# New order shifts for the projection stage and layer 1's attention of a two-layer decoder, and the compressed keys turned in four operations instead of eight

## The chip, the cores and the metric

The kernel runs on one core of a Trainium2 chip, as one execution with all inputs and the output in device memory. The metric is device time in microseconds (us). Before the change three runs gave a median of 2461.87 us (2460.61 to 2462.18).

A core has five engines that run at once, each through its own list of instructions in order: TensorE (PE, matmuls and transposes), VectorE (DVE), ScalarE (ACT), GpSimd (POOL), and SyncE (SP), which here issues the transfers between device memory and the core's on-chip memory. An instruction waits, on semaphores, until what it reads is written and what it overwrites is read; everything behind it on its engine waits with it. In the profile "PE busy" is matmul time, "PEclk" the TensorE clock that was granted (1.00 is full speed).

## The reference

A batch of one, 1024 tokens of width 1024, two layers, float32. Layer 0 is native sparse attention, layer 1 forgetting attention; each layer also has four heads that attend to 256 memory tokens, an output projection and a convolutional FFN (width 2816). Cut to what matters here:

```python
# layer 0: projections and the compressed keys
proj = h @ w_in                      # queries, 6 x 2 groups of keys/values, gates, memory queries
blocks = u[:, idx] + pos_emb         # 63 blocks of 32 tokens, stride 16
flat = blocks.transpose(...).reshape(B, n_cmp, G, L_CMP * dh)
compress = gelu(flat @ w1 + b1) @ w2 + b2
kc = rope(compress(k_cmp), cmp_end)  # rope: [x1*cos - x2*sin, x2*cos + x1*sin]
vc = compress(v_cmp)
# layer 1: forgetting attention, causal in chunks of queries
s = q @ k.T * scale + dcum[t] - dcum[s]
o = masked_softmax(s, causal) @ v
```

Then `x = x + concat(o_mix, o_mem) @ w_o`, `x = x + conv_ffn(rms_norm(x))` for each layer, and a last norm.

## The kernel before

**Arithmetic.** Every float32 operand of a projection is split into an upper and a lower part, and `mm3` (L320, matmuls at L324 to L326) forms upper x upper, upper x lower and lower x upper. The upper part of a weight is a copy on ACT, the lower a subtraction on DVE or POOL (tiles `wh`, `wl`, from `wr`, where the transfer lands; 3 `wr`, 4 pairs `wh`/`wl`). Products go to PSUM: two wide buffers `psa` (1024 columns) and four `psb` (512).

**Stages**, in us of the profiled span: 0 to 154 the projections of layer 0; 154 to 590 its attention; 590 to 1150 its output projection and FFN; 1150 to 1420 down projection, norm and layer 1's first projections; 1420 to 1780 layer 1's attention; 1780 to 2464 the output projection, FFN and final norm of layer 1.

**What sets the order.** The projection stage and the two attentions are lists of tasks given to class `Plan` (L50). A task names an engine, an assumed duration (for instance 1.36 us for six matmuls, 0.69 us for a 512-wide DVE product), the tasks it follows, the buffers it takes and gives back, and a priority. `Plan.run` walks through assumed time while the program is built: a free engine takes the ready task with the lowest priority number whose buffers are free. The sequence that comes out is written down as each engine's program and is not altered when the chip runs it. The table `SHIFT` adds half of its number, in the units of the priority, to single tasks:

```python
if self.auto and not key:
    key = ("t", len(self.tasks))
if key:
    prio += 0.5 * self.shift.get(key[0], {}).get(key[1], 0)
```

`SHIFT["p"]` belongs to the projection stage, with tasks by their number; `SHIFT[0]` and `SHIFT[1]` to the attentions of the layers, by a letter for the kind of task and the number of its unit (s0 scores, m0 row maxima, e0 exponentials, n0 normalising, t transposes of the probabilities, h and l their upper and lower parts, v values, d loads of queries, keys and values, f fillers: the projections of layer 1 that are still to be done, w their weights, x loads of the output projection's operand, y its weights).

**The projection stage** (`proj_tasks`) holds the normed input `hT` of both halves of the tokens, multiplies it with the columns for values, keys and queries, turns queries and keys by RoPE on DVE (L1170) and POOL, and has two side chains. `compress_tasks` (L1276) is called for kind 0 (keys) and kind 1 (values): a projection into `psa`, scaling on DVE (L1317), placing the blocks with their positions into `kk` (L1332 on DVE, L1327 on POOL), their split into `m` (L1338 ACT, L1341 DVE), 16 steps of `mm3` with the weights w1 (the 128x256 matmuls `psb<-m,wh`, weights split at L1360 and L1363), the bias (L1379, DVE, tile `ch`), gelu (L1389, ACT), two transposes (L1384, PE), the split into `cth` (L1391 ACT, L1392 DVE), the matmul with w2, and a bias (L1401, tile `cres`). For the keys follow `rotate()` (L1409 to L1417, eight DVE operations of 128x32, tiles `crt` and `cdup`) and a transpose (L1421). The memory tokens' keys and values (`mem_tasks`, weights at L1541 and L1544, split of the operand at L1527) and memory queries (`mem_queries`, scaled at L1470) run in between.

**Layer 1's attention** (`planned` with `l=1`) goes through units of one head and one half of the queries. A unit loads its keys (`kk`, `ky`), queries (`qq`, two buffers; `qx`, one buffer for each half of the queries, L2003) and values (`vv`), forms scores in `psa` (L409, two matmuls of each width: 64 rows with the head's numbers, 80 with decay), reads them on DVE (L439: adds the mask, finds the maximum, frees `psa`), takes exponentials on ACT (L452), normalises on POOL, transposes the probabilities (L523), splits them (L534 ACT, L537 DVE, tiles `pt`) and multiplies with the values (L547). Between these PE has fillers: the projections of layer 1's queries and keys (`psb<-hT,wh` and `psb<-wh,hT` of 128x512, six to a task), whose results go to device memory (`qd`, `kd`) and come back as queries and keys. Row sums of heads go out by `ob` (L668) and come back as the output projection's operand (`wr<-o`, L694).

## Time and profile before

| what | number |
|---|---|
| median of 3 runs | 2461.87 us (2460.61 to 2462.18) |
| profiled execution, its own time | 2465.3 us |
| its span, first to last instruction | 2463.5 us, mean granted clock 0.998 |
| PE busy | 2425.6 us, 98% of the span |
| DVE, ACT, POOL busy | 72%, 54%, 42% |
| projection stage (0 to 154 us) | PE busy 144.94 us, DVE 109.62, ACT 76.78, POOL 88.42 |
| layer 1's attention (1420 to 1780 us) | PE busy 351.56 us, DVE 198.15, ACT 209.52, POOL 173.00 |

A row of a stretch reads: its limits, its length, then PE, weight loads, DVE, ACT and POOL busy us with the number of instructions, the granted clock, the share of the transfer engines and GB/s. A row of a timeline reads: start, duration, engine, line, operation, output and inputs, shape, count, and in brackets the idle time before it with what ended it. A row of waits reads: engine, tile and line that waited, what it waited for, us in total, how often, the longest.

### The profile page before, as it was taken

The numbers are of one execution on the slowest core, as the hardware profiler recorded it, in microseconds if no ns is written. First come the engines' busy times: TensorE is split into PE (matmuls) and PEld (weight loads), VectorE is DVE, ScalarE is ACT, GpSimd is POOL, SyncE is SP. The second block draws the span as 40 slices with busy tenths as digits, with TensorE's granted clock in tenths as the row PEclk, the third lists the DMA queues.
The fourth block names the chain that finished last, engine by engine and source line by source line (L and its number), as shares of the span: only waits on it lengthen the run. The fifth ranks groups of instructions, "written<-read, shape, count | busy, mean of one in ns | idle before, by whom it ended". The sixth has DMA issues, their size and how long they took to land.

```text
span 2463.5 us, 35014 instructions
## 1 busy us (share of the span) xinstructions
PE 2425.6 (98%) x12233; PEld 2042.4 (83%) x12233; DVE 1767.5 (72%) x2785; ACT 1330.4 (54%) x2466; POOL 1027.7 (42%) x964
## 2 busy tenths in 40 slices
PE   9989999999999999999999999999999999999998
PEld 8878888887888888888889888887778888888887
DVE  5888887875867887887665346556577878788766
ACT  5468887883444554454454256666345544444444
POOL 3765654782344554510003245437234545541001
PEclk9999999999999999999999999999999999999999
DMA  8772243556223333385335559568622333339423
GB/s 310 247 241 95 86 131 104 175 161 224 94 90 98 99 112 98 111 304 166 95 122 171 169 168 259 170 187 267 215 86 86 113 97 111 104 97 317 167 90 127
DMA packets 271888, 379.76 MB, mean 154 GB/s; under 512 B 24050, under 2 KB 139602, under 8 KB 271682
## 3 DMA queue, kind: packets, MB, share of 16 engines
q1 hardware_dynamic: 271712, 377.53, 47.2%
q8 instruction: 96, 1.57, 0.3%
q14 instruction: 80, 0.66, 0.1%
HBM read 256.67 MB, written 122.16 MB: 154 GB/s over the span
## 4 chain that ended last, share of the span: by engine, by line
PE 89%; DMA 4%; DVE 3%; ACT 2%; issue 1%; POOL 1%; SPq 0%; POOLq 0%; ACTq 0%; DVEq 0%
PE psa L324 13%; PE psa L325 13%; PE psa L326 13%; PE psb L324 10%; PE psb L326 10%; PE psb L325 10%; PE psa L409 6%; PE psb L523 6%; PE psb L547 6%; DMA qx<-qd 1%; PE psb L1768 1%; DVE pt L537 0%; DMA wr<-in_w_mem_kv_dram 0%; DVE m L1527 0%; DMA wr<-o 0%
## 5 line engine op out<-in xcount | busy, mean ns | idle before, releaser
L2349 DVE SCALAR_TENSOR_TENSOR v<-u,cw,v 128x1023 f32<-128x1023 f32 (+1 forms) x176 | 273.9, 1556 | 68.7 <-ACT v L2347 68.5
L537 DVE TENSOR_TENSOR pt<-psb,pt 128x512 fp32r<-128x512 f32 (+2 forms) x380 | 243.1, 660 | 67.7 <-ACT pt L534 62.3
L2347 ACT ACTIVATE v<-u,cw 128x1024 f32<-128x1024 f32 x88 | 109.6, 1246 | 310.2 <-DVE u L2336 297.1
L245 ACT ACTIVATE wh<-wr 128x512 fp32r<-128x512 f32 (+1 forms) x202 | 147.1, 729 | 233.2 <-PE psa L326 121.7
L547 PE MATMUL psb<-pt,vv 128*128 128x512 f32 (+2 forms) x864 | 262.6, 363 | 3.3 <-DVE pt L537 3.0
L534 ACT ACTIVATE pt<-psb 128x512 fp32r<-128x512 f32 (+2 forms) x380 | 212.4, 575 | 92.6 <-PE psb L523 72.7
L246 DVE TENSOR_TENSOR wl<-wr,wh 128x512 fp32r<-128x512 f32 (+1 forms) x202 | 186.6, 925 | 94.7 <-ACT wh L245 94.4
L292 POOL TENSOR_TENSOR rs<-ss,consts 128x1 f32<-128x1 f32 x28 | 17.1, 611 | 519.1 <-DVE ss L290 519.1
L324 PE MATMUL psa<-hT,wh 128*128 128x512 f32 x592 | 231.1, 391 | 0.1
L325 PE MATMUL psa<-hT,wh 128*128 128x512 f32 x592 | 230.4, 389 | 0.0
L326 PE MATMUL psa<-hT,wl 128*128 128x512 f32 x592 | 230.4, 389 | 0.0
L409 PE MATMUL psa<-kk,qq 128*128 128x512 f32 (+4 forms) x792 | 175.0, 336 | 6.8 <-DVE stat L439 2.2
L439 DVE CUSTOM_DVE_ANT_0 ps<-psa,caub 128x128 f32<-128x128 f32 (+1 forms) x192 | 139.1, 750 | 39.8 <-PE psa L409 32.2
L2242 POOL TENSOR_TENSOR ws<-wr 128x512 f32<-128x512 f32 x44 | 75.1, 1708 | 216.9 <-DMA wr<-in_w_up_dram 185.8
L452 ACT ACTIVATE ps<-ps,stat 128x128 f32<-128x128 f32 (+1 forms) x192 | 148.0, 775 | 32.4 <-DVE stat L439 31.9
L547 PEld LDWEIGHTS psb<-pt,vv 128*128 128x128 f32 x864 | 147.8, 189 | 18.1 <-DVE pt L537 4.4
L523 PE MATMUL psb<-consts,ps 128*128 128x128 f32 x928 | 145.0, 275 | 3.3 <-DVE pt L537 1.5
L324 PE MATMUL psa<-hx,wh 128*128 128x512 f32 x368 | 144.0, 392 | 0.4 <-ACT u L2339 0.4
L325 PE MATMUL psa<-hx,wh 128*128 128x512 f32 x368 | 143.6, 390 | 0.0
L326 PE MATMUL psa<-hx,wl 128*128 128x512 f32 x368 | 143.3, 389 | 0.0
L409 PEld LDWEIGHTS psa<-kk,qq 128*128 128x128 f32 x792 | 125.0, 191 | 22.1 <-DVE stat L439 6.2
L324 PE MATMUL psb<-wh 128*128 128x512 f32 x352 | 137.4, 390 | 0.1
(360 smaller groups left out, 6928.2 us busy)
## 6 DMA issues: line engine op xcount, KB each, us to landing
wr<-in_w_up_dram SPq DMA_DIRECT2D x88, 512.0 KB, 3.8
wr<-gd SPq DMA_DIRECT2D x154, 256.0 KB, 2.9
gd<-v SPq DMA_DIRECT2D x88, 256.0 KB, 2.1
qq<-qd SPq DMA_DIRECT2D x72, 256.0 KB, 4.0
gd<-gs SPq DMA_DIRECT2D x66, 256.0 KB, 2.3
o<-ob SPq DMA_DIRECT2D x64, 256.0 KB, 2.6
wr<-o SPq DMA_DIRECT2D x32, 512.0 KB, 6.5
hT<-in_w_down_dram SPq DMA_DIRECT2D x64, 256.0 KB, 5.4
```

The costliest lines, as they stand in the source:

```text
L245: nc.scalar.activation(hi, src, AF.Copy)
L246: (low or nc.vector).tensor_tensor(lo, src, f32(hi), ALU.subtract)
L324: mm(out, lh, rh, start=first, stop=False, skip_group_check=more)
L325: mm(out, lh, rl, start=False, stop=False, skip_group_check=more)
L326: mm(out, ll, rh, start=False, stop=last, skip_group_check=more)
L409: nc.tensor.matmul(out, w, rhs, start=b not in banks[:i], stop=b not in banks[i + 1:])
L452: nc.scalar.activation(p, p, AF.Exp, bias=st[:, 0, ii:ii + 1], scale=-1.0, accum_out=st[:, 1, ii:ii + 1])
L523: nc.tensor.transpose(tp[0:kb, x:x + P], br["pt"][ii][:, o:o + kb], self.ident)
L534: self.nc.scalar.activation(st["hi"], st["src"], AF.Copy)
L537: self.nc.vector.tensor_tensor(st["lo"], st["src"], f32(st["hi"]), ALU.subtract)
L547: self.nc.tensor.matmul(u["o"][:, iis[0] * P:iis[0] * P + w], br["v"](j), t[:, x:x + w], start=st["begin"] and first and i == 0, stop=st[" ...
L2349: nc.vector.scalar_tensor_tensor(v[:, d:], u[:, :S - d], cw[:, tap, i:i + 1], v[:, d:], ALU.mult, ALU.add)
```

## The change

Two things are edited.

1. `SHIFT["p"]["t"]` and `SHIFT[1]` are replaced as a whole: 39 shifts of the projection stage by 37 others, those of layer 1's attention, 58 of them, by 66 others. `SHIFT[0]` stays, and so does the order of layer 0's attention and of all that isn't planned.
2. `rotate()` forms the same four products and two results with four DVE operations in place of eight: each of them is 64 elements wide and reads some operands twice by broadcast. The planner's assumed cost for it (3.5 us) is not edited.

```diff
             def rotate():
-                k1, k2 = res[:, 0:32], res[:, 32:64]
-                dve.tensor_tensor(t[:, 0], k1, ct[:, 0], ALU.mult)
-                dve.tensor_tensor(t[:, 1], k2, ct[:, 1], ALU.mult)
-                dve.tensor_tensor(t[:, 2], k2, ct[:, 0], ALU.mult)
-                dve.tensor_tensor(t[:, 3], k1, ct[:, 1], ALU.mult)
-                for d in range(2):
-                    dve.tensor_tensor(dup[:, d, 0:32], t[:, 0], t[:, 1], ALU.subtract)
-                    dve.tensor_tensor(dup[:, d, 32:64], t[:, 2], t[:, 3], ALU.add)
+                k = res.rearrange("p (h f) -> p h f", h=2)
+                for i in range(2):
+                    dve.tensor_tensor(t[:, 2 * i:2 * i + 2], k, ct[:, i:i + 1].to_broadcast([P, 2, 32]), ALU.mult)
+                for h, op in enumerate((ALU.subtract, ALU.add)):
+                    dve.tensor_tensor(dup[:, :, 32 * h:32 * h + 32], t[:, h:h + 1].to_broadcast([P, 2, 32]), t[:, 3 - h:4 - h].to_broadcast([P, 2, 32]), op)
...
-    SHIFT = {"p": {"t": {11: -24, 23: -4, 41: 15, 48: 3, 56: 13, 69: 3, 76: 25, 95: 19, 100: -30, ...
+    SHIFT = {"p": {"t": {8: -40, 26: -9, 53: 3, 56: 26, 84: 14, 86: -14, 100: -5, 113: 10, 115: 5, ...
...
-             1: {"d": {2: 6, 6: 4, 18: 3, 28: -17},
-                 "e0": {12: 15, 13: 15, 28: -8},
...
+             1: {"d": {0: 8, 1: 6, 6: 14, 18: 3, 27: -8, 28: -20, 29: -15},
+                 "e0": {13: 2, 18: 24},
...
```

Lines behind L1417 move up by three, and behind the table by two. In the rows below a number behind a name is that of a buffer or of the n-th tile of the name, and has no meaning between the two kernels.

**DVE around the bias of the compressed keys** (L1379, tile `ch`) and their split (L1392, `cth`), about 105 to 121 us of the span before. Before:

```order
L1170 TENSOR_TENSOR qq_87_1013<-psa_171,cos_693 128x512
L1527 SCALAR_TENSOR_TENSOR m_80_865<-xl_800,gcol,m_79_864 128x256 x2
L988 TENSOR_TENSOR st_493<-rt_86_995,st_493 128x512
L1544 TENSOR_TENSOR wl_285<-wr_146,wh_284 128x1024
L1341 TENSOR_TENSOR m_91_1082<-kk_84_947,m_90_1081 128x1024
L1379 TENSOR_TENSOR ch_1091<-psb_192,cb_108 128x256
L1332 TENSOR_TENSOR kk_94_1111<-vv_856,cpos_116 64x8x63 x2
L1392 TENSOR_TENSOR cth_1092<-psb_192,cth_1092 128x256
```

and after:

```order
L1541 TENSOR_TENSOR wl_258<-wr_132,wh_257 128x1024
L1170 TENSOR_TENSOR qq_87_1017<-psa_190,cos_688 128x512
L1379 TENSOR_TENSOR ch_1052<-psb_172,cb_108 128x256
L1341 TENSOR_TENSOR m_91_1050<-kk_84_946,m_90_1049 128x1024
L1541 TENSOR_TENSOR wl_154<-wr_151,wh_153 128x1024
L1332 TENSOR_TENSOR kk_94_1061<-vv_904,cpos_116 64x8x63 x2
L988 TENSOR_TENSOR st_533<-rt_86_998,st_533 128x512
L1392 TENSOR_TENSOR cth_1053<-psb_171,cth_1053 128x256
L1363 TENSOR_TENSOR wl_258<-wr_161,wh_257 128x1024
L1341 TENSOR_TENSOR m_91_1050<-kk_94_1061,m_90_1049 128x1024
L1401 TENSOR_TENSOR cres_111<-psb_172,cb_108 128x64
L1412 TENSOR_TENSOR crt<-cres_111,ct 128x64 x2
L1414 TENSOR_TENSOR cdup<-crt 128x2x32 x2
```

The subtraction L988, the weight split of the memory keys (L1544, now L1541) and the split L1341 stood ahead of L1379 and now stand behind it, ahead of L1392 (of two weight splits ahead of L1379 one is left there). The last two rows are the new `rotate()`.

**PE around the transposes of the compressed keys** (L1384). Before, where `psb<-m,wh` of 128x256 are the memory tokens' projection and `psb<-hT,wh` of 128x512 the memory queries:

```order
L326 MATMUL psb_194<-wh_257,m_80_865 128x256
L324 MATMUL psb_195<-hT_91,wh_165 128x512
L325 MATMUL psb_195<-hT_92,wh_165 128x512
L326 MATMUL psb_195<-hT_91,wl_166 128x512
L324 MATMUL psb_195<-hT_91,wh_165 128x512
L325 MATMUL psb_195<-hT_92,wh_165 128x512
L326 MATMUL psb_195<-hT_91,wl_166 128x512
L1384 MATMUL psb_192<-consts,ch_1091 128x128 x2
L324 MATMUL psb_195<-hT_91,wh_165 128x512
```

and after:

```order
L326 MATMUL psb_172<-wh_153,m_77_850 128x256
L324 MATMUL psa_137<-hT_93,wh_314 128x512
L325 MATMUL psa_137<-hT_94,wh_314 128x512
L326 MATMUL psa_137<-hT_93,wl_315 128x512
...
L326 MATMUL psa_137<-hT_93,wl_315 128x512
L1384 MATMUL psb_171<-consts,ch_1052 128x128 x2
L324 MATMUL psb_173<-m_78_853,wh_257 128x256
L325 MATMUL psb_173<-m_79_854,wh_257 128x256
L326 MATMUL psb_173<-m_78_853,wl_258 128x256
```

Twelve 512-wide matmuls of another projection now stand between the last w1 matmul of the keys and the transposes, and the memory tokens' projection, 48 matmuls of it, comes behind the transposes, ahead of the matmul with w2.

**PE in layer 1's attention**, at the place where the projections that run as fillers have just ended (about 1678 us before). Before, the filler of the output projection (`psb<-wh,hT`) stands ahead of and inside the unit's scores:

```order
L547 MATMUL psb_12703<-pt_12974,vv_15047 128x256 x2
L324 MATMUL psb_12637<-wh_15201,hT_15161 128x512
...
L326 MATMUL psb_12637<-wh_15201,hT_15162 128x512
L409 MATMUL psa_12854<-kk_15324,qq_1499_15378 128x128
L409 MATMUL psa_12854<-ky_12618,qx_12616 128x128
L409 MATMUL psa_12854<-kk_15324,qq_1499_15378 128x256
L409 MATMUL psa_12854<-ky_12618,qx_12616 128x256
L409 MATMUL psa_12854<-kk_15324,qq_1499_15378 128x384
L409 MATMUL psa_12854<-ky_12618,qx_12616 128x384
L324 MATMUL psb_12637<-wh_15383,hT_15161 128x512
```

and after, from the same kind of value matmul to the first such filler:

```order
L547 MATMUL psb_12699<-pt_12970,vv_14907 128x256 x2
L409 MATMUL psa_12850<-kk_14820,qq_1487_15137 128x128
...
L409 MATMUL psa_12850<-ky_12615,qx_12612 128x384
L409 MATMUL psa_12872<-kk_14820,qq_1487_15137 128x512
L409 MATMUL psa_12872<-ky_12615,qx_12612 128x512
L409 MATMUL psa_12850<-kk_14820,qq_1490_15184 128x512
L409 MATMUL psa_12850<-kk_14820,qq_1490_15184 128x128
...
L409 MATMUL psa_12850<-ky_12615,qx_12613 128x384
L324 MATMUL psb_12708<-wh_15080,hT_15068 128x512
```

Twenty score matmuls of two units now stand in a row. They fill five wide PSUM buffers one after the other (128+256+384 columns, 512, 640, 768, 896), of which there are two; then 24 matmuls of the filler follow at once.

More of the change, by code (lines that the diff above doesn't have):

```diff
@@ L2045 @@
     RATE = (330.0, 300.0)
-    SHIFT = {"p": {"t": {11: -24, 23: -4, 41: 15, 48: 3, 56: 13, 69: 3, 76: 25, 95: 19, 100: -30, 101: -36, 104: 7, 115: 20, 124: -28, 127: 15, 160: 32, 200: -6, 208: 9, 245: -3, 246: -5, 258: 11, 301: -21, 305: 28, 313: 18, 377: -6, 381: 1, 389: -40, 400: 8, 404: -24, 407: 12, 415: 6, 433: 40, 442: -31, 449: -40, 465: 5, 468: -8, 476: -13, 495: 9, 496: -8}},
+    SHIFT = {"p": {"t": {8: -40, 26: -9, 53: 3, 56: 26, 84: 14, 86: -14, 100: -5, 113: 10, 115: 5, 119: -15, 124: -9, 132: -16, 146: -10, 150: -29, 160: 11, 200: -28, 207: 23, 208: 19, 209: 30, 242: 26, 243: -28, 258: 31, 266: 17, 267: 2, 268: 10, 293: -19, 324: -16, 327: -21, 362: 40, 384: -15, 407: -40, 421: 39, 462: 16, 479: -4, 487: 24, 488: 30, 499: 25}},
              0: {"e0": {24: -17, 25: -9},
```

21 rows, old and new, of the table SHIFT are left out of this document.

## The prediction

> **What bounds the kernel now.** First the busy times of the page.
>
> ```profile
> PE 2425.6 (98%) x12233; PEld 2042.4 (83%) x12233; DVE 1767.5 (72%) x2785; ACT 1330.4 (54%) x2466; POOL 1027.7 (42%) x964
> ```
>
> PE works 2425.6 of the span's 2463.5 us, and the change leaves every matmul in place: it can only alter the 38 us in which PE stands still, and the clock at which it runs. Which part of these 38 us is in reach is told by the table of stretches (length, then PE, weight loads, DVE, ACT and POOL busy, clock, transfers), for the two stages whose order is new:
>
> ```profile
> 0.00:154.00 154.00, 144.94 (x813) 126.48 (x813) 109.62 (x136) 76.78 (x120) 88.42 (x71) 1.00 0.81 280
> 1420.00:1780.00 360.00, 351.56 (x1896) 294.94 (x1896) 198.15 (x404) 209.52 (x464) 173.00 (x193) 1.00 0.70 212
> ```
>
> 9.1 us of standstill in the first and 8.4 us in the second: 17.5 us are the most that any order could win back here, 0.7% of the time. The rest of the program keeps its order. What PE waits for, from the view of its waits in the projection stage,
>
> ```profile
> PE psb L1384 <- ACT ch L1389: 2.1, 1, 2.1
> PE psb L1421 <- DVE st L1470: 1.7, 1, 1.7
> PE psa L324 <- ACT hT L1009: 1.4, 1, 1.4
> PE psa L325 <- DVE hT L1012: 0.3, 1, 0.3
> ```
>
> and in layer 1's attention:
>
> ```profile
> PE psb L547 <- DVE pt L537: 2.1, 3, 1.2
> PE psa L409 <- DMA qq<-qd: 1.7, 1, 1.7
> PE psb L523 <- DVE xh L738: 1.3, 1, 1.3
> PE psa L409 <- ACT ob L668: 0.9, 1, 0.9
> PE psb L324 <- ACT ob L668: 0.7, 1, 0.7
> PE psa L409 <- DMA qx<-qd: 0.3, 1, 0.3
> ```
>
> These are single waits of 0.3 to 2.1 us, each with another cause. In the second list the three for `pt`, the one for `qq` and the one for `qx` all lie between 1671 and 1683 us, 4.1 us in a cluster.
>
> **The change part by part.** *First transposes (L1384).* DVE's timeline before them:
>
> ```profile
> 110.57 1.29 DVE L988 TENSOR_TENSOR st<-rt,st 128x512 fp32r<-128x512 f32 x1 [0.41 <-ACT st L1184]
> 111.78 2.31 DVE L1544 TENSOR_TENSOR wl<-wr,wh 128x1024 fp32r<-128x1024 f32 x1
> 114.01 2.31 DVE L1341 TENSOR_TENSOR m<-kk,m 128x1024 fp32r<-128x1024 f32 x1
> 116.24 0.41 DVE L1379 TENSOR_TENSOR ch<-psb,cb 128x256 f32<-128x256 f32 x1
> 116.69 3.52 DVE L1332 TENSOR_TENSOR kk<-vv,cpos 64x504 f32<-64x504 f32 x2
> 120.23 0.42 DVE L1392 TENSOR_TENSOR cth<-psb,cth 128x256 fp32r<-128x256 f32 x1
> ```
>
> DVE is in a run without a pause: L1379 is late since three operations stand ahead of it, 1.29 + 2.31 + 2.31 = 5.9 us, which the new order puts behind it. PE arrives earlier too, by 24 matmuls of the memory projection and six of the memory queries that no longer stand ahead, priced by their distance from start to start:
>
> ```profile
> 113.51 0.40 PE L324 MATMUL psb<-hT,wh 128*128 128x512 f32 x1
> 113.74 0.40 PE L325 MATMUL psb<-hT,wh 128*128 128x512 f32 x1
> ...
> 117.16 0.44 PE L1384 MATMUL psb<-consts,ch 128*128 128x128 f32 x2 [2.10 <-ACT ch L1389]
> ...
> 118.83 0.28 PE L324 MATMUL psb<-m,wh 128*128 128x256 f32 x1
> 118.94 0.28 PE L325 MATMUL psb<-m,wh 128*128 128x256 f32 x1
> ```
>
> 24 x 0.117 + 6 x 0.23 = 4.2 us. The new wait is 2.1 + 4.2 - 5.9 = 0.4 us, and less if the keys' first projection ends one six-matmul step (six of 0.23, 1.4 us) earlier, as the order has it. Bounds 0 to 0.4; I take 0: **-2.1 us**.
>
> *What is late next: the split `cth` (L1392).* The three operations are not gone. In the new order DVE does L1379, then L1341, the weight split, L1332 twice, L988 and only then L1392, on which the matmul with w2 waits, and behind it on PE all that follows. By the rows above that is 0.41 + 2.31 + 2.31 + 3.52 + 1.29 + 0.42 = 10.3 us. The same shapes go faster where they meet nobody:
>
> ```profile
> 103.84 1.22 DVE L1363 TENSOR_TENSOR wl<-wr,wh 128x1024 fp32r<-128x1024 f32 x1
> ...
> 107.20 0.68 DVE L1170 TENSOR_TENSOR qq<-psa,cos 128x512 f32<-128x512 f32 x1
> ```
>
> With 1.22 for the two 1024-wide ones and 0.68 for L988 it is 7.5 us. PE meanwhile starts the transposes 0.92 us after L1379 (116.24 to 117.16), spends about 0.3 us on them and 48 x 0.117 = 5.6 us on the memory projection: 6.8 us. A wait of 0.7 to 3.5 us; half way between, since the slow prices come from a time with POOL busy and I cannot tell how much of POOL is left there: I take **+1.7 us**. It holds up the second projection and the memory queries behind it on PE, nothing on the other engines that isn't waiting for DVE anyway.
>
> *The rotation.* Two of its eight operations, and what POOL did meanwhile:
>
> ```profile
> 122.45 0.23 DVE L1401 TENSOR_TENSOR cres<-psb,cb 128x64 f32<-128x64 f32 x1
> ...
> 126.85 1.28 DVE L1411 TENSOR_TENSOR crt<-cres,ct 128x32 f32<-128x32 f32 x1
> ...
> 129.31 0.18 DVE L1413 TENSOR_TENSOR crt<-cres,ct 128x32 f32<-128x32 f32 x1
> ```
>
> ```profile
> 126.51 5.44 POOL L43 TENSOR_TENSOR wl<-wr,wh 128x512 fp32r<-128x512 f32 x4 [0.66 <-DMA wr<-in_w_mem_kv_dram]
> ```
>
> From 126.85 to 132.12 us the eight took 5.3 us: four of 1.27 to 1.33 us, as long as one of POOL's four pieces (5.44/4 = 1.36), and four of 0.18. A small DVE operation here either costs its own 0.2 us or stands until POOL's piece is done. Four operations of the doubled width cost 4 x 0.23 = 0.9 us free (the row of that width), at most 4 x 1.33 = 5.3 us. This is DVE time; on the path stands only the transpose L1421, whose wait of 1.7 us was for it. The new order puts L1421 behind the first scores of layer 0, several microseconds later, so that either price is covered by these scores: **-1.7 us** (bounds -1.7 and 0; if the scores' own masks are late behind the rotation, the wait is paid there). The Trainium skill, page "SBUF — State Buffer", section "Who interferes with whom", says that DVE and GpSimd hold a shared port pair for a whole instruction and the loser fully blocks; by it the number of operations counts and not their size, so up to half of the 5.3 us would go. The two groups of durations agree with it; the sum is the same by both, since L1421 has cover either way.
>
> *The start.* Values come first in the new order, whose weight piece is 584 wide in place of 1024. The wait for `hT` (L1009, 1.4 us) is that of the first rows' arrival and stays; of the 0.3 us for L1012 I take **-0.3 us** (bounds -0.3 and +1.4, one more wait of the same kind).
>
> Projection stage: -2.1 + 1.7 - 1.7 - 0.3 = **-2.4 us**.
>
> *Layer 1's attention.* Here nearly every row moves and no walk by hand covers them all. The cluster costs more than its 4.1 us, as short stretches after it show:
>
> ```profile
> 1682.00:1683.80 1.80, 1.50 (x6) 1.36 (x7) 0.00 (x0) 0.07 (x1) 1.80 (x3) 0.64 1.01 365
> 1683.80:1685.60 1.80, 1.80 (x6) 1.41 (x6) 1.12 (x6) 1.16 (x5) 1.80 (x2) 0.50 1.08 352
> ...
> 115.00:117.10 2.10, 0.05 (x1) 0.00 (x0) 2.07 (x3) 0.41 (x1) 2.10 (x2) 1.00 1.04 394
> ```
>
> The granted clock falls to 0.64 and 0.50: 1.8 x 0.36 + 1.8 x 0.5 = 1.5 us lost. After the single 2.1 us wait at 115 us it stays at 1.00. So a cluster of waits can halve the clock for some 3 us. The Trainium skill, page "TensorE: Matmul & The Clock Gate", section "🔬 Part 1: The HAM clock gate (the "warmup" mystery)", puts the halving after at least one idle window of about 3.4 us; no single wait here is as long, so by that page the cluster would cost 4.1 us alone. This trace differs from it; the 1.5 us stand.
>
> The cluster is 4.1 + 1.5 = 5.6 us. In the new order the twenty scores use keys loaded long ahead, and their query load on SP no longer stands directly behind the fresh keys' load, which speaks for it going; the values for `pt` ahead of it keep their place, and the filler between is less. Bounds 0 and -5.6; I take half, **-2.8**. The three other waits, 1.3 + 0.9 + 0.7 = 2.9 us, are tied to places that moved; bounds 0 and -2.9, half again, **-1.5**.
>
> Against that stands the run of twenty scores in two PSUM buffers. The third buffer's matmuls need the first read by L439, the fourth the second, the fifth the third:
>
> ```profile
> 1656.11 0.29 DVE L439 CUSTOM_DVE_ANT_0 ps<-psa,caub 128x128 f32<-128x128 f32 x1
> ...
> 1656.67 0.55 DVE L439 CUSTOM_DVE_ANT_0 ps<-psa,caub 128x384 f32<-128x384 f32 x1
> ...
> 1657.15 0.69 DVE L439 CUSTOM_DVE_ANT_0 ps<-psa,caub 128x512 f32<-128x512 f32 x1
> ...
> 1664.94 0.81 DVE L439 CUSTOM_DVE_ANT_0 ps<-psa,caub 128x640 f32<-128x640 f32 x1
> ```
>
> DVE reads the first three widths in 1657.15 - 1656.11 = 1.04 us (0.55 of it for the last, 384 wide, which can't start before it is written), then 512 in 0.69 and 640 in 0.81. At 0.23 us for 512 columns and two matmuls for each width PE issues the buffers in 0.69 (768 columns), 0.46, 0.58, 0.69 and 0.81 us, and a matmul ends 0.40 - 0.23 = 0.17 us behind that. The first buffer is read at 0.69 + 0.17 + 0.55 = 1.41 us, PE was ready for the third at 1.15: 0.26 us; the second is read at 1.41 + 0.69 = 2.10, PE ready for the fourth at 1.41 + 0.58 = 1.99: 0.11; the third at 1.99 + 0.17 + 0.81 = 2.97 (2.10 is earlier), PE ready for the fifth at 2.79: 0.18. That is 0.6 us with DVE free; one other 512-wide operation between the reads, as stand there in the program, adds 0.68: **+1.3 us** (bounds 0, where reads and writes overlap better than this, and 2.6, three such operations).
>
> Stage: -2.8 - 1.5 + 1.3 = **-3.0 us**. Together -2.4 - 3.0 = **-5.4 us**: the profiled execution's 2465.3 us becomes 2459.9; the median of the runs shown lies 3.4 us below that execution, and from it the forecast is 2461.87 - 5.4 = **2456.5 us**, 0.22% less.
>
> **The rivals.** *A: the waits only move.* The waits before are each from a different engine; a new order that was chosen by assumed durations has waits of its own wherever DVE's 2.31 in place of 1.22 us shows that durations depend on what runs beside. For it: the `cth` wait above. Against it: two removed waits have a plain cause that is gone. Then attention stays as it was and the projection stage keeps its -2.4: 2459.5 us; with the upper bound of the `cth` wait (+1.8) 2461.3. This is also the case in which the change doesn't do what it says.
>
> *B: queries late in layer 1 (slower).* `qx` has one buffer for each half. In the new order the load for the unit after the twenty scores can be issued only when their first group has read it, and stands on SP behind a load of `wr`. Rows of SP and of the chain of waits:
>
> ```profile
> 1657.39 1.15 SPq L729 DMA_DIRECT2D xh<-xd  x2
> 1662.75 2.44 SPq L694 DMA_DIRECT2D wr<-o  x2
> ...
> 1675.57 6.83 DMA qx<-qd
> ```
>
> SP stood 1662.75 - 1658.54 = 4.2 us before such a `wr` load, and a `qx` load took 6.83 us to land. From the end of the first group that is 11.0 us, while PE has the other four buffers (2.5 us and 1.3 of waits) and 24 fillers (5.5 us): 9.3 us. It waits 1.7 us, and with the clock's 1.5 us it is 3.2 at one place; at the three reloads behind the fillers' end 9.6. With the cluster staying (+2.8 on the forecast): -5.4 + 2.8 + 9.6 = +7.0, 2468.9 us at three places, 2465.7 at two. It decides from the point at which such a load lands over 9.3 us behind the group. Against it: SP's wait may be far shorter, as `wr` has three buffers. By the clock gate's rule no wait here would halve the clock, and two places would make 2462.7 us.
>
> *C: most waits go.* Cluster and the other three all go (-2.8 - 1.5 more), the scores' run costs nothing (-1.3): -5.4 - 5.6 = -11.0, 2450.9 us. For it: PE has 98% already and DVE is idle 45% of that stage. Against: a new order of 1900 matmuls with no wait of its own.
>
> **How the numbers follow.** Forecast 0.38, A 0.28, B 0.19, C 0.15. What a measurement of this kernel can tell from no change is about 0.2%, 4.9 us: faster is below 2457.0, slower above 2466.8. The forecast lies half a microsecond inside faster; with the unknowns of the `cth` wait (+1.8, -1.0), the scores' run (+1.3, -1.3) and the halves of the attention (+-4.3) its own range is 2452 to 2461, a little over half faster (0.21 of 0.38). C is faster (0.15), A with a stroke of C 0.05. Slower is B at three places and a little of A: 0.15. Faster 0.41, same 0.44, slower 0.15. The range leaves a tenth on each side: from C's 2451 less 1, to B between two and three places: 2450 to 2467.
>
> **What would show it.** In the new profile: no wait of L1384 for `ch`, and L1392 as the releaser of a wait of 0.7 to 3.5 us near 105 to 120 us; no wait at the transpose of the turned keys; four rotation operations of 0.23 us or about 1.3 each and none between; in layer 1's attention waits of L409 for L439 inside a run of twenty scores with 24 fillers behind it, and no stretch there with a clock under 0.9. Wrong would be: a wait on `qq` or `qx` of over 1.5 us behind those fillers (B), a standstill of more than 17 us over both stages together, or a difference in stages whose order is unchanged of more than the 3.4 us by which one profile differs from the median.

## The result, and the profile after

The changed kernel takes **2481.28 us** (median of 4 runs, 2479.59 to 2484.01) against 2462.02 us (4 runs, 2460.61 to 2463.12): a ratio of 1.0071, 95% interval 1.0059 to 1.0083 (the quotient of the two medians, 1.0078, lies inside it). It is 19.3 us slower by the medians, 0.8%. The forecast was 2456.5 us with a range up to 2467: wrong in its sign.

The profiled execution took 2479.99 us. Its page begins with

```profile
span 2478.2 us, 35009 instructions
PE 2434.3 (98%) x12233; PEld 2047.1 (83%) x12233; DVE 1755.9 (71%) x2781; ACT 1328.5 (54%) x2466; POOL 1027.1 (41%) x964
```

TensorE (PE) runs the same 12233 matmuls and is *busy* 8.7 us longer (2425.6 before), with a mean granted clock of 0.995 for 0.998. Only 6.0 us of the 14.7 us by which the span grew are standstill (2478.2 - 2434.3 = 43.9 us, 37.9 before). Of the 8.7 us of busy time, 6.6 are matmuls at a lower clock: while PE worked, half clock cost 10.0 us after and 3.4 before. The other 2.1 us are matmuls that follow each other more slowly at full clock.

Where: both profiles run the same order of matmuls except in the two stages, so that the start of the n-th matmul can be compared. The changed kernel is 0.9 us ahead at the 400th matmul and 4.6 behind at the 800th (both inside the projection stage, where the orders differ), 3.0 at the 1200th (behind that stage), 1.4 at the 7200th (ahead of layer 1's attention) and 15.4 at the 9200th (behind it). At the end it is 14.7. So it loses some 3 to 5 us in the projection stage and 14 us in layer 1's attention.

The waits of PE after, in the projection stage,

```profile
PE psb L324 <- DVE cth L1392: 3.7, 1, 3.7
PE psb L326 <- DVE cth L1392: 2.3, 1, 2.3
PE psa L324 <- ACT rm L1084: 1.1, 1, 1.1
```

and in layer 1's attention:

```profile
PE psa L409 <- DMA qx<-qd: 3.7, 4, 2.5
PE psb L547 <- DVE pt L537: 2.2, 5, 0.8
PE psa L409 <- DMA qq<-qd: 2.0, 2, 1.2
PE psa L409 <- DVE stat L439: 1.9, 3, 0.9
PE psb L523 <- POOL ps L491: 1.8, 4, 0.8
PE psb L547 <- ACT pt L534: 0.9, 2, 0.6
```

The waits of before for L1384 and L1421 are gone, as forecast. Two others stand in their place, both for `cth`. The keys' matmul with w2 waits 2.3 us; the memory queries wait 3.7 us for the PSUM buffer that the values' `cth` split frees, which before was a wait of the same split of 1.5:

```profile
PE psb L324 <- DVE cth L1392: 1.5, 1, 1.5
```

In layer 1 nothing was won: the waits for loads of queries cost 5.7 us (2.0 before), and two releasers are new, the reads L439 that free PSUM and the normalisations L491 on GpSimd (POOL).

The clock after, in stretches behind the two `cth` waits:

```profile
118.00:120.00 2.00, 0.96 (x5) 0.96 (x5) 2.00 (x3) 1.22 (x2) 2.00 (x3) 0.76 0.31 115
120.00:122.00 2.00, 2.00 (x6) 1.61 (x6) 2.00 (x2) 0.00 (x0) 2.00 (x2) 0.50 1.01 256
122.00:124.00 2.00, 2.00 (x9) 1.81 (x9) 1.97 (x3) 0.00 (x0) 2.00 (x2) 0.50 0.93 299
124.00:126.00 2.00, 2.00 (x12) 2.00 (x12) 1.97 (x3) 0.00 (x0) 2.00 (x3) 0.53 0.68 270
...
146.00:148.00 2.00, 1.81 (x5) 1.44 (x6) 2.00 (x9) 0.90 (x1) 0.00 (x0) 0.59 1.00 319
148.00:150.00 2.00, 2.00 (x7) 1.59 (x6) 1.22 (x6) 1.97 (x4) 1.25 (x1) 0.56 0.91 338
```

About 3.2 us are lost in the first of them (0.2 + 1.0 + 1.0 + 0.9) and 1.6 in the second; before, no half clock fell into this stage. The standstill of the stage hardly grew: its waits add up to 9.0 us before and 10.1 after. In layer 1 the clock halves twice (from 1521.9 and from 1682.4 us): busy time by the clock that was missing, 4.9 us are lost there, 1.7 before.

The stretches of layer 1's attention after, and the same bounds before:

```profile
1420.00:1500.00 80.00, 77.22 (x404) 64.51 (x404) 33.07 (x71) 39.68 (x91) 36.29 (x41) 1.00 0.64 186
1500.00:1600.00 100.00, 96.70 (x539) 81.01 (x538) 57.62 (x121) 64.76 (x152) 47.66 (x56) 0.98 0.55 166
1650.00:1700.00 50.00, 43.68 (x212) 33.98 (x211) 26.40 (x62) 30.02 (x64) 27.19 (x29) 0.93 0.76 226
```

```profile
1420.00:1500.00 80.00, 79.36 (x417) 66.28 (x417) 36.97 (x83) 43.18 (x99) 37.61 (x43) 1.00 0.66 192
1500.00:1600.00 100.00, 98.73 (x574) 84.43 (x573) 61.09 (x130) 68.72 (x160) 52.67 (x63) 1.00 0.68 199
1650.00:1700.00 50.00, 46.15 (x246) 37.92 (x245) 31.37 (x65) 33.16 (x70) 35.39 (x36) 0.97 0.82 253
```

There are 2.1, 2.0 and 2.5 us more standstill in these three, and a lower clock in two of them; from 1600 to 1650 us it is 0.2 more and from 1700 to 1795 us 0.4 less. So the loss has several places. It isn't the run of twenty scores alone.

From the start of the 7200th matmul to that of the 9200th the stage takes 396.1 us after and 382.1 before. Of the 14.0 us, 6.5 are standstill (14.95 for 8.44), 3.2 are half clock (4.9 for 1.7), and 4.3 are left: matmuls at full clock that follow each other more slowly (376.3 for 372.0). The fillers don't, at 0.23 us from start to start; the attention's own matmuls do, the transposes at 0.095 us for 0.090 and the scores with the head's numbers at 0.201 for 0.193. The modelled ends of neighbouring matmuls overlap, so part of these 4.3 us may be waits too short to show as standstill; the trace doesn't tell.

### The profile page after: what moved, and what is told of

It reads as the page before. It is cut to its first block, busy times and chain, and to the rows that moved or that the text cites. A ratio compares the mean times of both kernels' runs of the same rounds, so it can differ in the third digit from the quotient of the medians.

```text
span 2478.2 us, 35009 instructions
## 1 busy us (share of the span) xinstructions
PE 2434.3 (98%) x12233; PEld 2047.1 (83%) x12233; DVE 1755.9 (71%) x2781; ACT 1328.5 (54%) x2466; POOL 1027.1 (41%) x964
## 4 chain that ended last, share of the span: by engine, by line
PE 87%; DMA 5%; DVE 3%; ACT 2%; issue 1%; POOL 1%; SPq 0%; POOLq 0%; ACTq 0%; DVEq 0%
PE psa L324 13%; PE psa L325 13%; PE psa L326 13%; PE psb L324 10%; PE psb L326 10%; PE psb L325 10%; PE psa L409 6%; PE psb L547 6%; PE psb L523 5%; DMA qx<-qd 1%; DMA vv<-in_x_dram 1%; PE psb L1765 1%; DVE pt L537 1%; ACT pt L534 0%; DMA x<-xh 0%
## 5 line engine op out<-in xcount | busy, mean ns | idle before, releaser
L537 DVE TENSOR_TENSOR pt<-psb,pt 128x512 fp32r<-128x512 f32 (+2 forms) x380 | 242.3, 660 | 67.9 <-ACT pt L534 57.7
L439 DVE CUSTOM_DVE_ANT_0 ps<-psa,caub 128x128 f32<-128x128 f32 (+1 forms) x192 | 139.1, 750 | 46.0 <-PE psa L409 38.2
L523 PE MATMUL psb<-consts,ps 128*128 128x128 f32 x928 | 146.0, 276 | 4.0 <-POOL ps L491 1.8
```

Source lines behind the costliest of these rows:

```text
L523: nc.tensor.transpose(tp[0:kb, x:x + P], br["pt"][ii][:, o:o + kb], self.ident)
L537: self.nc.vector.tensor_tensor(st["lo"], st["src"], f32(st["hi"]), ALU.subtract)
```

## The experiments

### Which part: each alone

Four kernels: the one before with the new projection shifts alone; with the new layer 1 shifts alone; with the new rotation alone; and with projection shifts and rotation.

```diff
-    SHIFT = {"p": {"t": {11: -24, 23: -4, ...     # old table
+    SHIFT = {"p": {"t": {8: -40, 26: -9, ...      # new table: projection stage alone
...
-             1: {"d": {2: 6, 6: 4, ...
+             1: {"d": {0: 8, 1: 6, ...            # new table: layer 1 alone
```

> The kernel before with the new shifts of the projection stage alone (old rotation, old layer 1). Theory (projection and layer 1 both lose, apart from each other): the aligned traces put the changed kernel 3.0 us behind at the 1200th matmul and 1.5 us at the 6000th, so 1.5 to 5 us slower than before. Rival (all of the loss was in layer 1, the projection stage is noise from one profile to the next): within 1 us of before.

> The kernel before with the new shifts of layer 1's attention alone. Theory: the loss sits in that stage's own order, 13 to 15 us slower than before. Rival (it takes over a disturbance from the earlier stages, as when the transfers left over differ): under 8 us slower.

> The kernel before with the four-operation rotation alone. Theory: two to three microseconds of VectorE time saved ahead of the transpose that waits 1.7 us, so 1 to 1.9 us faster, if nothing else becomes late. Rival (each of the four runs against GpSimd and costs 1.3 us each): same within 1 us.

> New projection shifts and new rotation, old layer 1: the changed kernel without the layer 1 part. Theory (rotation has cover in the new order): equal to the kernel with the projection shifts alone within 1 us. Rival (rotation lies on the path): 1 to 2 us faster than that one.

| kernel | median us | ratio to before (2462.3 us, 21 runs) | 95% interval |
|---|---|---|---|
| projection shifts alone | 2467.11 | 1.0019 | 1.0010 to 1.0029 |
| layer 1 shifts alone | 2476.28 | 1.0060 | 1.0045 to 1.0075 |
| rotation alone | 2462.01 | 1.0001 | 0.9992 to 1.0011 |
| projection shifts and rotation | 2466.97 | 1.0021 | 1.0007 to 1.0034 |

The parts add up: 4.8 + 14.0 = 18.8 us of the 19.3, and the rotation is worth nothing that these runs can show, in either order. Its operations did become cheap where POOL is at rest. The rotation's tiles with the rotation alone (least, median and longest ns of each):

```profile
L1412 DVE TENSOR_TENSOR crt<-cres,ct x2: 214/214/214, 123.9 to 124.0; 128x64 f32<-128x64 f32 x2
L1414 DVE TENSOR_TENSOR cdup<-crt x2: 218/221/224, 124.3 to 124.4; 128x64 f32<-128x64 f32 x2
```

and in the changed kernel, with POOL at work beside them:

```profile
L1412 DVE TENSOR_TENSOR crt<-cres,ct x2: 1057/1184/1310, 123.3 to 124.2; 128x64 f32<-128x64 f32 x2
L1414 DVE TENSOR_TENSOR cdup<-crt x2: 210/713/1216, 125.6 to 126.7; 128x64 f32<-128x64 f32 x2
```

0.9 us in the one, 3.8 in the other, for the old eight's 5.3. With the rotation alone, the wait of 1.7 us at L1421 is gone from its profile and yet the time is the same: the expected 1 to 1.9 us did not come. The values' `cth` wait there is 2.0 for 1.5 us, and the clock halved twice in this stage (from 115.0 and from 145.7 us), behind two waits that had cost no clock before (below).

### The two `cth` waits

In the projection shifts alone, the splits were put sooner on VectorE (DVE) by hand in the finished order:

```diff
+        if self.auto:
+            by = {t["id"]: t for t in order}
+            for a, b in [(255, 254), (433, 315), (486, 433), (436, 486)]:   # put task a right behind task b
+                order.remove(by[a])
+                order.insert(order.index(by[b]) + 1, by[a])
```

> New projection shifts alone, with the two splits L1392 put sooner on VectorE: the keys' one ahead of the two placings L1332 and of L988, the values' one ahead of six of the eight operations L1524 and the cast L1638; nothing else moved. Theory (these two splits cost the projection stage its loss: waits of 2.3 and 3.7 us and about 4.6 us of half clock behind them): 2459 to 2463 us against 2467.1, the first wait gone, the second 1.5 us or less. Rival (what stood ahead of the splits is wanted as urgently, the wait goes over to the placed blocks): 2466 to 2468 us, with a new wait of the same size.

2465.90 us, ratio 1.0013 (1.0002 to 1.0025), where the shifts alone had 1.0019: inside each other's intervals, 1.2 us by the medians and not the 4 to 8 us of the theory. Its waits (line numbers are 5 higher):

```profile
PE psb L329 <- DVE cres L1406: 3.1, 1, 3.1
PE psa L414 <- DMA qq<-qd: 2.3, 2, 2.0
PE psb L329 <- DVE cth L1397: 1.3, 1, 1.3
```

The keys' `cth` wait went and came back one step on, for `cres` (L1401), which on DVE stands behind what was passed, the two placings (4.0 us together) and a subtraction (1.6 us), and behind a weight split and a split of 2.3 us each that stood ahead of it already. That is the rival. The values' wait fell from 3.7 to 1.3 us as expected, and the first scores of layer 0 waited 2.3 us for their queries, where the shifts alone had 0.6. In this profiled execution no half clock fell into the stage at all, and still the runs are not clearly faster.

### Does the standstill cost the clock?

In the projection shifts alone, 20 matmuls of 128x256 whose product is thrown away fill the place where PE waits for the keys' `cth`:

```diff
         def second():
-            x["o"] = self.psb()[:, 0:HD]
+            ps = self.psb()
+            x["o"] = ps[:, 0:HD]
             th = x["th"]
+            for _ in range(20 if kind == 0 else 0):
+                nc.tensor.matmul(ps[:, 0:256], h[0][0][:, 0, 0:P], h[0][0][:, 0, 0:256], start=True, stop=True)
```

> New projection shifts alone, with 20 more matmuls of 128x256 on finished data (their product is thrown away) directly ahead of the keys' matmul with w2, where TensorE stands 2.3 us for L1392. Theory (the clock halves because TensorE stands still there): the clock stays at 1.00 from 118 to 126 us, the lost 3 to 3.6 us come back, the extra 2.3 us of matmuls fit in the wait: 2463.5 to 2465 us against 2467.1. Rival (the half clock comes from elsewhere, or the wait isn't TensorE's alone): 2467 to 2469.5 us and a half clock at the same place.

2464.87 us, ratio 1.0005 (0.9995 to 1.0015): with 2.3 us of additional work it is 2.2 us faster than the shifts alone by the medians. The intervals just overlap, so that this gain is likely and not settled. The added matmuls, and the clock in the stretches behind them, of that kernel:

```profile
117.62 2.56 PE L1399 MATMUL psb<-hT 128*128 128x256 f32 x20
```

```profile
120.00:122.00 2.00, 2.00 (x14) 1.75 (x13) 2.00 (x2) 0.31 (x1) 2.00 (x2) 1.00 0.66 246
122.00:124.00 2.00, 2.00 (x18) 1.96 (x17) 2.00 (x2) 0.00 (x0) 2.00 (x2) 1.00 1.08 236
```

The clock stays at 1.00 where it was 0.50. So the half clock is a consequence of the standstill, and at some 3.2 us it had cost more than the wait of 2.3 us itself. A later wait, for queries (2.7 us for 0.6), then halved it at 137 us (0.75 and 0.50). Up to the same matmul behind the stage the two profiled executions take 220.2 and 220.1 us: what was won at this place was lost at the next one. The number came as expected, but these two profiles don't show it coming by the way that was expected.

The length of a wait alone doesn't decide. The clock record of the traces has half clock in all 16 profiled executions, apart from their starts and ends, in pieces of 3.41 us, one to three in a row, and within one execution all pieces start on one grid of 3.41 us. Here is the same wait of 2.1 us at L1384, in stretches of that grid, first in the kernel before, then in the one with the rotation alone:

```profile
112.37:115.78 3.41, 2.68 (x18) 2.08 (x16) 3.41 (x2) 2.41 (x3) 2.75 (x3) 1.00 1.01 344
115.78:119.20 3.42, 2.04 (x12) 1.78 (x13) 3.38 (x4) 1.43 (x3) 3.42 (x3) 1.00 0.99 388
119.20:122.61 3.41, 3.41 (x32) 3.41 (x31) 3.35 (x4) 1.05 (x2) 3.33 (x3) 1.00 0.90 307
```

```profile
111.60:115.01 3.41, 1.30 (x8) 0.91 (x7) 3.38 (x3) 0.80 (x2) 3.41 (x4) 1.00 1.04 399
115.01:118.43 3.42, 3.42 (x15) 3.13 (x14) 3.37 (x4) 1.06 (x1) 3.35 (x3) 0.50 0.93 320
```

In the one, the grid cuts the wait into 0.73 and 1.38 us and nothing is lost; in the other, 2.11 us lie in one stretch and the next runs at half clock, which costs 1.7 us. The wait of 3.1 us for `cres` in the experiment before was cut into 1.37 and 1.70 us, and the clock stayed at 1.00 (122 to 128 us). Over all 16 traces, of the stretches at full clock with 1.0 to 1.4 us of standstill none of 73 is followed by half clock, with 1.4 to 1.6 us 3 of 23, with 1.6 to 1.9 us 14 of 18, and with more than that 36 of 37. So here it took about half of a 3.41 us stretch standing still, in one piece or several. The Trainium skill, page "TensorE: Matmul & The Clock Gate", section "🔬 Part 1: The HAM clock gate (the "warmup" mystery)", has an activity window of about 3.4 us that runs freely. The grid of these traces agrees with it. That one whole window must be idle, as its table has it, does not fit: 1.9 us of standstill in it were enough. The grid lies differently against the program in each execution, so the same wait can cost 1.7 us or nothing from run to run; how much of the difference between runs of one kernel this is, was not shown.

### Layer 1: single waits

The run of twenty scores begins, in the changed kernel, with the longest of the waits. The chain of waits, and SyncE (SP) and PE around it:

```profile
1673.06 8.57 DMA qx<-qd
```

```profile
1672.20 0.33 SPq L2000 DMA_DIRECT2D qx<-qd  x1
1672.63 0.38 SPq L694 DMA_DIRECT2D wr<-o  x1
1673.06 0.42 SPq L2000 DMA_DIRECT2D qx<-qd  x1
```

```profile
1681.67 0.33 PE L409 MATMUL psa<-ky,qx 128*128 128x128 f32 x1 [2.51 <-DMA qx<-qd]
```

The load that the first group needs is the last of three on SP, behind the other unit's and behind a `wr` load, and takes 8.57 us to land, with three transfers of 512 KB asked for shortly before. In the layer 1 shifts alone this one load was put seven transfers sooner (the move is written as above, task 1304 behind 1303).

> New layer 1 shifts alone, with one transfer moved on SyncE: the load of qx for the first unit of the run of twenty scores, put seven transfers sooner, behind the qq of its unit. Theory (this load is late because it stands behind two wr loads and another unit's queries): its wait of 1.4 to 2.6 us ahead of the run goes and with it most of 3 us of half clock; 2472 to 2474 us against 2476.3. Rival (the clock halves and the waits come for L439 or POOL all the same): 2475 to 2477 us.

2473.31 us, ratio 1.0033 (1.0021 to 1.0045) where the shifts alone had 1.0060 (1.0045 to 1.0075): 3.0 us back by the medians, as expected, and 6.6 by the ratios, whose intervals just touch. The half clock at 1677 us went with the wait; a piece of the same length stands at 1485 us in this execution. Of the waits between 1640 and 1700 us, that for `qx` falls from 1.8 to 0.5 us, and those for PSUM and for the normalisations stay:

```profile
PE psa L414 <- DVE stat L444: 2.4, 4, 0.9
PE psb L528 <- POOL ps L496: 0.9, 3, 0.4
PE psa L414 <- DMA qx<-qd: 0.5, 1, 0.5
```

Then all loads of queries were put directly behind the task they have to wait for:

```diff
+        at = {t["id"]: i for i, t in enumerate(order)}
+        for t in [t for t in order if t.get("q")]:          # loads of qq and qx
+            order.remove(t)
+            order.insert(1 + max([order.index(d) for d in t["deps"]], default=at[t["id"]] - 1), t)
```

> New layer 1 shifts alone, with every load of queries (qq, qx) of that stage put on SyncE directly behind the task it has to wait for. Theory (the planner's 2.6 us of delay plus 0.5 to 0.9 us is short of the 5 to 8.6 us that these loads take, so the new order asks for them too late; their waits add up to 8 us): 2466 to 2470 us against 2476.3. Rival (SyncE then stands at loads whose buffers are still in use, and keys and weights come late instead): 2476 us or slower.

2490.22 us, ratio 1.0103 (1.0088 to 1.0119): 14 us slower still by the medians. This theory falls. `qq` is waited for as without it (3.6 us, 3.4 with the layer 1 shifts alone), and now other things are late too:

```profile
PE psb L551 <- ACT pt L538: 5.8, 4, 2.8
PE psa L413 <- DMA qq<-qd: 3.6, 2, 2.6
PE psa L413 <- DMA ky<-kd: 2.1, 3, 1.0
```

At last one POOL operation was put behind the four normalisations it stood ahead of (task 1591 behind 1225), beside the load.

> New layer 1 shifts with the load of qx put sooner as in the run before, and on POOL one subtraction of the output projection's operand (L703, 1.3 us) put behind the four normalisations (L491) that it stood ahead of. Theory (this operation delays the normalisations for which three transposes wait 1.7 us together): these waits fall to 0.5 us or less, 1 to 1.5 us faster than with the load alone, 2471.8 to 2472.3 us against 2473.3. Rival (the transposes then wait for the next slowest, the exponentials on ScalarE or the PSUM buffers): within 0.5 us of the load alone.

2472.64 us, ratio 1.0044 (1.0028 to 1.0059): the same as with the load alone, within the intervals. The wait moved one instruction on, from L523 to the values, which now wait for L537 (L542 there):

```profile
PE psb L552 <- DVE pt L542: 1.3, 2, 1.1
PE psb L528 <- POOL ps L496: 0.4, 1, 0.4
```

### The same by hand in the old order

To see whether single waits can be taken out of the kernel before: with the rotation, the bias L1379 goes directly behind the last w1 step, and the loads of unit 28 of layer 1 go ahead of two `wr` loads (tasks 251 behind 248; 1394, 1395, 1396 behind 1393).

> The kernel before with the four-operation rotation, and two moves by hand: the bias L1379 of the compressed keys directly behind the last w1 step on VectorE, ahead of a weight split and a split of placed blocks; and on SyncE the loads of ky, qq and qx for unit 28 of layer 1 put ahead of two wr loads. Theory (single waits can be taken out one at a time where what is put back has cover): the wait of 2.1 us at L1384 falls to 0.6 us or less, the one of 1.7 us for qq to 0.5 or less and its half clock goes, 2457.5 to 2460 us against 2462.2. Rival (each such wait moves on to the next place, as in the changed kernel): 2461 to 2464 us.

2466.65 us, ratio 1.0016 (1.0007 to 1.0024): slower, above what either side expected. Both waits that were aimed at went, and others came. Between 1640 and 1700 us the weights of the output projection are now late (L715 and L718 in the numbers of before). In the projection stage the first scores of layer 0 waited longer for L439, and the wait at the transpose of the turned keys (L1428 there, 1.7 us before), which the rotation alone had removed, is back:

```profile
PE psb L334 <- ACT wh L725: 1.3, 1, 1.3
PE psb L533 <- POOL ps L501: 1.1, 1, 1.1
PE psb L335 <- DVE wl L728: 0.8, 1, 0.8
```

```profile
PE psa L419 <- DVE stat L449: 3.5, 1, 3.5
PE psb L334 <- DVE cth L1402: 2.3, 2, 1.4
PE psb L1428 <- DVE st L1477: 2.1, 1, 2.1
```

### Layer 1: how the fillers are spread

No single wait explains 14 us. In the new order the projections of layer 1 that fill PE's waits are bunched: from start to start of such matmuls, stretches of over 7 us without one add up to 85.6 us in the profile before (the longest 15.7) and to 127.1 after (24.3 us from 1664 on, and 27.1 from 1719 on). Four kernels have the old table with one group of the new layer 1 shifts each.

```diff
-             1: {"d": {2: 6, 6: 4, 18: 3, 28: -17}, ...
+             1: {"d": {0: 8, 1: 6, 6: 14, 18: 3, 27: -8, 28: -20, 29: -15}, ...    # here: group d alone
```

> The kernel before, in layer 1's table only the groups w, x and y new (weights of the fillers, operand and weights of the output projection). By the matmuls' order its stretches of over 6 us of attention work without a filler add up to 54 us, against 43 in the kernel before and 68 with the whole new table. Theory (time goes with that sum, 14.0 us for 24.4 us, 0.57 each): about 6 us slower than before. Rival (no relation): anywhere from 0 to 15 us, not in order of the sums over the four runs.

> The kernel before with only group d new in layer 1's table (loads of queries, keys and values). Stretches without a filler add up to 68 us. Theory (time goes with that sum): about 14 us slower than before. Rival (no relation; the loads are asked for in another order, which alone decides): anywhere from 0 to 15 us, not in order of the sums.

> The kernel before with only group f new in layer 1's table (the fillers). Stretches without a filler add up to 60 us, the longest 17. Theory (time goes with that sum): about 9 us slower than before. Rival (no relation): anywhere from 0 to 15 us, not in order of the sums.

> The kernel before with the groups s0, m0, e0, n0, t, h, l and v new in layer 1's table (scores to values). Stretches without a filler add up to 86 us. Theory (time goes with that sum): about 24 us slower than before, the slowest of the four. Rival (no relation): anywhere from 0 to 15 us, not in order of the sums.

| new groups in layer 1's table | median us | ratio to before (95% interval) | stretches without filler, by the order and in the trace, us | longest in the trace, us |
|---|---|---|---|---|
| none (before) | 2461.03 to 2462.46 | 1 | 43, 86 | 16 |
| w, x, y | 2467.01 | 1.0020 (1.0010 to 1.0029) | 54, 101 | 16 |
| f | 2475.68 | 1.0056 (1.0039 to 1.0073) | 60, 111 | 32 |
| d | 2472.61 | 1.0049 (1.0034 to 1.0064) | 68, 134 | 32 |
| all | 2476.28 | 1.0060 (1.0045 to 1.0075) | 68, 125 | 27 |
| s0, m0, e0, n0, t, h, l, v | 2478.56 | 1.0071 (1.0056 to 1.0086) | 86, 145 | 20 |

Expected by the sums were 6, 9, 14 and 24 us for w/x/y, f, d and the softmax group; measured are 0.20%, 0.56%, 0.49% and 0.71%, that is 4.9, 13.8, 12.1 and 17.5 us. (The sums measured in the traces include the waits themselves; those by the order don't.) Least and most are where they were expected, and the two in the middle are the other way about and within each other's intervals. The sum goes with the time, but it isn't a price: 18 us more of it cost 3 to 5 in the last step. And all four are slower than before, whichever group is new, so the runs don't separate "long stretches without a filler" from "any of these orders away from the one before". Nor does a group have a price of its own: the four alone cost 48 us together, and all of them at once 14. How a stretch without filler would cost is argued from the waits and not shown: there each step of the softmax chain, each PSUM buffer and each load that is late by half a microsecond stands on PE, whoever the releaser is. The slowest of them has its longest wait yet elsewhere:

```profile
PE psb L324 <- ACT wh L715: 3.7, 1, 3.7
```

Putting fillers into the longest stretches of the new order by hand, which would settle it, wasn't tried: the PSUM buffer of the last ones passes on to work that stands ahead of the place.

## Why the prediction was wrong, point by point

- **What bounds the kernel** was right: PE, which lost its time by standstill. Wrong was to take the 38 us of standstill as all that an order can move. The clock moved 6.6 of the 8.7 us by which PE's busy time grew, and the prediction let it move only in layer 1's cluster. Its own sign of being wrong, over 17 us of standstill in both stages together, came: 10.3 us up to 160 us and 15.0 us from 1420 to 1790 us.
- **First transposes, -2.1 us:** right, the wait is gone.
- **The split `cth`, +1.7 us (0.7 to 3.5):** the mechanism and the place were right and the wait 2.3 us. Both sides of the difference came out longer than summed, which left it inside its bounds: DVE took 11.1 us from the start of L1379 to the end of L1392 (7.5 to 10.3 summed, without two waits of 0.5 and 0.6 for ACT), and PE was ready 8.9 us after that start (6.8 summed). That the forecast of this wait held is in part luck. Missing was the clock behind it, about 3.2 us: the step took the row of 115 us, where 2.1 us had cost no clock, as a rule. That wait was cut by the clock's grid; the same wait in another run was not, and cost it.
- **The rotation, -1.7 us:** L1421 waits no longer, and each operation costs what was bounded (0.21 or 1.1 to 1.3 us). But the runs with the rotation alone show that the 1.7 us are not gained. In their profile the values' `cth` wait grew by 0.5 us and two pieces of half clock, 1.7 us each, fell into the stage; that these took the gain is likely and not shown.
- **The start, -0.3 us:** the profile after has 1.1 us for `hT` where 1.4 and 0.3 stood, and L1084 a new wait of 1.1 us. Nothing of the 0.3 us is left.
- **What the sum left out in the projection stage:** the values' `cth` wait, 1.5 us before and not named, became 3.7 us plus some 1.6 of clock. The sum had the waits that it named go or come, and the unnamed ones stay. Projection stage: forecast -2.4, measured +4.8 (the shifts alone).
- **Layer 1, -3.0 us: the step that failed most.** It took half of the cluster and half of the other waits as won, without a row that said so, and as the only price the run of twenty scores. Measured +14.0 (the layer 1 shifts alone): in the two profiles 6.5 us more standstill, 3.2 us more at half clock and 4.3 us of matmuls that follow each other more slowly. "Half" stood for not knowing, and yet it leaned one way: a new order of 1900 matmuls takes old waits away and brings its own. The bounds, 0 to -5.6 and 0 to -2.9, held no loss at all. Only rival B held a loss there, and the range ended at 2467.
- **The run of twenty scores, +1.3 us:** the waits for L439 inside it are 0.5 us; the wait at its head was for `qx`, 2.5 us, and behind it the clock was halved to 1690 us. The sentence that its query load "no longer stands directly behind the fresh keys' load, which speaks for it going" looked at one neighbour on SP and not at the two `wr` loads and the other unit's queries.
- **Rival B** named the right resource, `qx` behind a `wr` load on SP with a load of 7 us (8.57 measured) and the clock's loss on top, at the wrong place (behind the fillers and not at the run's head). Moving that load gives back 3 us of the 14 by the medians (6.6 by the ratios), so B alone isn't the cause.
- **Rival A**, that the waits only move, is what the runs show again and again: with the splits put sooner, with the POOL operation put later, and in the old order mended by hand. It was priced as no change in the attention and at most as the upper `cth` wait in the projection stage; but a wait that moves can come out longer or with a half clock behind it.
- **The clock gate's rule** was weighed and the row preferred, rightly; the 1.5 us of the cluster are 1.7 by the clock record. But the row was then used at one place only.

What stays open: how much of layer 1's 14 us is due to bunched fillers and how much to the rest of the order. One load accounts for 3 to 7 of them; for the rest the runs show what PE lost, and not which part of the new order brought it.

## What to carry to other kernels

Where one engine is busy 98% of the time and what remains is many short waits with different releasers, a change of the order does not have the sum of those waits as its gain: here each wait that was taken away uncovered another, and bounds for the order of a whole stage must include a loss as large as the standstill that is there. Look at what the new order has where nothing independent is left to do: the stretches of the critical engine's work without a filler, added up in both orders before any wait is priced, put the mildest and the worst of the changed orders here in their places, though they gave no price. And a wait of two microseconds on TensorE is priced with the half clock that may follow it, 1.7 us for each 3.41 us of it.

## What the runs showed of the hardware that was not expected

- A wait of 2.1 to 2.3 us on TensorE can halve the granted clock for 3.4 or 6.8 us (119.1 to 125.9 us after), or leave it at 1.00 (115 us before; 3.1 us at 121 us with the splits put sooner). What decided in these traces was how much of the standstill fell into one stretch of a 3.41 us grid: 1.9 us or more halved the next stretch in 36 of 37 cases, less than 1.4 us in none of 73. Matmuls on finished data in the wait kept the clock at 1.00 at that place, and with 2.3 us more work the kernel was not slower.
- A transfer of 160 KB (`qx`) took 8.57 us from issue to landing with several of 256 and 512 KB ahead of it. Over its 24 loads the time was 4.0 to 7.9 us before (median 5.7) and 3.9 to 9.2 after (6.4). The planner's assumption is 0.53 + 2.6 us.
- Four DVE operations of 128x64 with two operands on chip took 0.21 to 0.22 us each alone, and 1.06 to 1.31 us (one 0.21) beside POOL operations of 1.29 to 1.75 us. At half the width four of the eight old ones had taken 1.27 to 1.33 us beside POOL: there an operation's width did not set its price.
